# Keys carried between chunks through DRAM, and a fifth place for weight pairs

## The chip, the cores and the metric

The kernel runs on one core of a Trainium2 chip. The metric is the device time of one execution in microseconds (us), the median of three runs. One more execution of the same program was recorded by the hardware profiler; every duration below comes from that recording.

The core's engines run side by side, each through its own instructions in a fixed order: TensorE (PE, with its weight loads as PEld), VectorE (DVE), ScalarE (ACT), GpSimd (POOL), and SyncE (SP), which here only issues DMAs. An engine that waits for something holds up all that stands behind it in its own order.

## The reference

Two decoder layers over one sequence of 2048 tokens of width 1024. Each layer projects the stream once and splits the result; a sliding-window attention group and a Mamba-2 group read it side by side; both are gated, joined by one output projection, added to the stream and normalized.

```python
def hybrid_layer(x, w_in, conv_w, conv_b, dt_bias, a_log, d_skip, ssm_norm_w, sinks, w_out, ln_g, ln_b):
    proj = jnp.einsum("bld,de->ble", x, w_in)
    q, k, v, z_attn, z_ssm, xbc, dt_raw = jnp.split(proj, IN_SPLITS, axis=-1)
    attn = sliding_window_attention(q, k, v, sinks) * jax.nn.silu(z_attn)
    xbc = jax.nn.silu(causal_depthwise_conv(xbc, conv_w, conv_b))
    ...
    y = ssd_chunked(xs, dt, a, bm, cm)
    ssm = gated_rmsnorm(y, z_ssm, ssm_norm_w)
    out = jnp.einsum("ble,ed->bld", jnp.concatenate([attn, ssm], axis=-1), w_out)
    return layer_norm(DEEPNORM_ALPHA * x + out, ln_g, ln_b)
```

In the attention, queries and keys stand in blocks of 128 tokens, and a block of queries sees its own block of keys and the one before it. There are 4 key/value heads of 64 numbers a token. So a block of 128 keys is needed once more by the block that follows.

## The kernel before

**Tiles and stages.** The sequence is cut into 4 chunks of 512 tokens (4 blocks of 128), and the program walks layer by layer, chunk by chunk. In a chunk come the value projection (`stage_v`), then, for each of two halves: keys (`stage_k`), queries and gate of two heads (`proj_a`), attention block by block (`mix_a`), the projections of the Mamba group (`proj_s`), the output projection of the attention half (`out_proj`), the chunked scan block by block (`mix_s`), and, a half later, the output projection of the scan's half (the `late` list).

**Split numbers.** Every large product is made in three matmuls of rounded parts: a number is split into a high and a low part, and high x high, high x low and low x high are added up. A weight tile is thus a pair: `wpair`, 128 partitions x 2 x 512 numbers, 4 KB on each partition. It takes part in 12 matmuls (of 512 columns, or 272 for the value weights) and is then done with.

**Where weights come from.** On first use a weight is loaded raw (`wr`), split by ACT and DVE and written to DRAM as a pair; layer 1's weights are split ahead of time during chunks 1 to 3 of layer 0 (`w_ahead`, one for every third pair used). All later uses load the finished pair by one DMA of 512 KB (`w_split`, line 126). These loads go into a pool of 4 places: the load of a pair waits until the last matmul has read the pair that had its place four pairs earlier.

**Keys.** `stage_k` makes two tiles `kt` of 128 partitions x 2 (high, low) x 640 columns: 128 columns of the chunk before and 512 of its own. The 128 old columns come from `kcar`, four tiles of 1 KB a partition that live through the whole program: POOL copies `kcar` in (line 321, in chunks 1 to 3), ACT copies the last 128 columns out for the next chunk (line 326, in every chunk).

**Order.** The kernel is written through a scheduler: the code says what depends on what, and the scheduler, which models times of its own, sets each engine's order. Any change in the pools can move instructions all over. All DMAs are issued by SP from one queue, in one order. In PSUM the tags decide who shares a bank: `ps_g` (the transposed result of a scan block) and `ps_s` (scores) share one single bank under tag "s"; the projections share 5 banks.

Of the kernel before, what the change touches and what calls it, by code (L numbers as in the profile page):

```python
# [23 lines left out]
F32 = mybir.dt.float32  # L24
F32R = mybir.dt.float32r
# [6 lines left out]
P = 128  # L32
# [3 lines left out]
CH = 512  # L36
NCH = SEQ // CH
# [5 lines left out]
WP = 512  # L43
# [12 lines left out]
def trunk(ctx, tc, a):  # L56
    nc = tc.nc
    PS = bass.MemoryType.PSUM

    const = ctx.enter_context(tc.tile_pool(name="const", bufs=1))  # L60
    lay = ctx.enter_context(tc.tile_pool(name="lay", bufs=2))
    xp = ctx.enter_context(tc.tile_pool(name="xp", bufs=1))
    wp = ctx.enter_context(tc.tile_pool(name="wp", bufs=1))
# [4 lines left out]
    dram = ctx.enter_context(tc.tile_pool(name="dram", bufs=1, space=bass.MemoryType.DRAM))  # L68
# [4 lines left out]
    def bank(pool, name):  # L73
        if pool is ps_pj:
            return pool.tile([P, 512], F32, name=name, tag="bank")
        tag = TAG[name]
        return pool.tile([P, 512], F32, name=name, tag=tag, bufs=NS if tag == "s" else 1)
# [6 lines left out]
    def w_load(src, n, t=None):  # L84
        if t is None:
            t = wp.tile([P, WP], F32, name="wr", bufs=4)
        t = t[:, 0:n]
        nc.sync.dma_start(out=t if len(src.shape) == 2 else t.rearrange("p (k n) -> p k n", k=src.shape[1]), in_=src)
        return t

    kcar = [const.tile([P, 2, P], F32R, name=f"kc{i}") for i in range(4)]
    state = [const.tile([P, 512], F32, name=f"st{i}") for i in range(2)]
    halo = const.tile([P, 12, 3], F32, name="halo")

# [12 lines left out]
    def w_parts(hs, ls, src, scale, eng):  # L107
        if scale is None:
            split(hs, ls, src, "act", eng)
        else:  # L110
            nc.scalar.activation(out=hs, in_=src, func=AF.Copy, scale=scale)
            nc.vector.scalar_tensor_tensor(out=ls, in0=src, scalar=scale, in1=hs.bitcast(F32),
                                           op0=ALU.mult, op1=ALU.subtract)

    def w_store(key, n):
        w_dram[key] = dram.tile([P, 2, n], F32, name="wd_" + "_".join(map(str, key)))
        return w_dram[key]

    def w_split(key, c, dsrc, n, scale=None, pool=False, dst=None):

        if dst is None:
            dst = wp.tile([P, 2, WP], F32R, name="wpair", bufs=4)
        d = dst[:, :, 0:n]
        hs, ls = d[:, 0], d[:, 1]
        if key in w_dram:
            nc.sync.dma_start(out=d.bitcast(F32), in_=w_dram[key])
            cnt["use"] += 1
            if cnt["use"] % 3 == 0 and ahead:
                w_ahead(*ahead.pop(0))
            return hs, ls  # L130
        src = w_load(dsrc, n)
        cnt["w"] += pool
        w_parts(hs, ls, src, scale, nc.gpsimd if pool and cnt["w"] % 2 == 0 else nc.vector)
        if key[1] > 0 or not on_use(key):
            nc.sync.dma_start(out=w_store(key, n), in_=d.bitcast(F32))
        return hs, ls

    def on_use(key):
        return key[0] == "o" and key[2] > 1

    def w_ahead(key, dsrc, n, scale):

        src = w_load(dsrc, n)
        hi = wp.tile([P, WP], F32R, name="whi", tag="wr", bufs=4)[:, 0:n]
        w_parts(hi, src, src, scale, nc.vector)
        dst = w_store(key, n)
        nc.sync.dma_start(out=dst[:, 0], in_=hi.bitcast(F32))
        nc.sync.dma_start(out=dst[:, 1], in_=src)
# [80 lines left out]
    def proj_cm(X, L, i, ps, pool=True):  # L229
        for half in range(2):  # L230
            wh, wl = w_split(("cm", L, i, half), X.c, a["wcm"][L, i][:, half * 4:half * 4 + 4, :], 512, pool=pool)
            for kk in range(4):
                k = half * 4 + kk
                xh, xl = X[k]
                s = slice(kk * P, (kk + 1) * P)
                nc.tensor.matmul(out=ps, lhsT=wh[:, s], rhs=xh, start=(k == 0), stop=False)  # L236
                nc.tensor.matmul(out=ps, lhsT=wh[:, s], rhs=xl, start=False, stop=False)  # L237
                nc.tensor.matmul(out=ps, lhsT=wl[:, s], rhs=xh, start=False, stop=(k == KT - 1))  # L238
# [9 lines left out]
    def stage_v(L, X):  # L248
        banks = [bank(ps_acc, "ps_v") for _ in range(NB)]
        for k in range(KT):  # L250
            X[k]
            wh, wl = w_split(("v", L, k), X.c, a["wvdt"][L][:, k, :], 272)
            proj_tok(X, [t[:, 0:272] for t in banks], k, wh, wl)
        return banks
# [56 lines left out]
    def stage_k(L, c, pr, X):  # L311
        ps = bank(ps_cm, "ps_k")
        proj_cm(X, L, pr, ps, pool=False)
        kts = []
        for i in range(2):
            kv = 2 * pr + i
            kt = ap_.tile([P, 2, P + CH], F32R, name="kt", bufs=2)
            kf = kt.bitcast(F32)
            s, o = (slice(0, 64), slice(64, 128)) if i == 0 else (slice(64, 128), slice(0, 64))
            if c > 0:  # L320
                nc.gpsimd.tensor_copy(out=kt[:, :, 0:P], in_=kcar[kv].bitcast(F32))
            nc.scalar.copy(out=kt[s, 0, P:], in_=ps[s])
            nc.vector.tensor_tensor(out=kt[s, 1, P:], in0=ps[s], in1=kf[s, 0, P:], op=ALU.subtract)
            nc.scalar.copy(out=kt[o, 0, P:], in_=ps[s])
            nc.vector.tensor_copy(out=kt[o, 1, P:], in_=kf[s, 1, P:])
            nc.scalar.copy(out=kcar[kv], in_=kf[:, :, CH:CH + P])
            kts.append(kt)
        return kts

# [122 lines left out]
    def out_proj(L, c, grp, mixt, racc, evac, nw=None, pre=None, dhs=2):  # L452
        for dh in range(dhs):
            if pre is not None:
                pre(dh)
            banks = [bank(ps_acc, "ps_out") for _ in range(NB)]
            for e in range(4):
                wh, wl = w_split(("o", L, grp, dh, e), c, a["wo"][L, grp, dh][:, e, :], 512,
                                 None if nw is None else nw[:, e:e + 1])
                for b in range(NB):  # L460
                    mh, ml = mixt[b][:, 0, e, :], mixt[b][:, 1, e, :]
                    nc.tensor.matmul(out=banks[b], lhsT=mh, rhs=wh, start=(e == 0), stop=False)  # L462
                    nc.tensor.matmul(out=banks[b], lhsT=mh, rhs=wl, start=False, stop=False)  # L463
                    nc.tensor.matmul(out=banks[b], lhsT=ml, rhs=wh, start=False, stop=(e == 3))  # L464
            for b in range(NB):
                evac(b, racc[b][:, dh * 512:(dh + 1) * 512], banks[b])
# [251 lines left out]
    for L in range(DEPTH):  # L718
# [3 lines left out]
        for c in range(NCH):  # L722
# [7 lines left out]
            for half in range(2):  # L730
                kts = stage_k(L, c, half, X)
                qs, zs = proj_a(L, half * 2, X)
                flush()
                if half == 0:
                    racc = load_res(L, c)
                mixt = new_mixt()
                mix_a(L, lc, c, half * 2, vr, vprev, kts[0], qs, zs, mixt)
                qs, zs = proj_a(L, half * 2 + 1, X)
                mix_a(L, lc, c, half * 2 + 1, vr, vprev, kts[1], qs, zs, mixt)
                o = proj_s(L, lc, c, half, X, d)  # L740
                pre = None
                if half == 1 and (L, c) != (DEPTH - 1, NCH - 1):
                    Xn = XLoad(L + (c + 1) // NCH, (c + 1) % NCH)
                    pre = Xn.half
                out_proj(L, c, half, mixt, racc, ev_alpha if half == 0 else ev_add, pre=pre)
                mixt = new_mixt()
                rstd = mix_s(L, lc, c, half, d, o, mixt)

                def tail(L=L, c=c, half=half, mixt=mixt, racc=racc, rstd=rstd, lc=lc):
                    end = half == 1 and L == DEPTH - 1 and c == NCH - 1  # L750
                    nw = lc["nw"][:, half * 4:half * 4 + 4]
                    out_proj(L, c, 2 + half, mixt, racc, ev_rstd(rstd), nw, dhs=1 if end else 2)
                    if end:
                        last_out(L, c, 2 + half, mixt, racc, rstd, nw)
                    elif half == 1:
                        norm_store(L, c, racc)

                late.append(tail)
# [60 lines left out]
```

## Time and profile before

| | |
|---|---|
| median of 3 runs | 3217.2 us (3206.6, 3217.2, 3219.31) |
| profiled execution, whole | 3223.33 us |
| profiled execution, span from first to last instruction | 3221.6 us |
| TensorE busy | 3112.8 us (97%) |
| mean granted TensorE clock | 0.989 of full speed |
| DVE / ACT / POOL busy | 2165.2 / 1451.0 / 1241.2 us |
| DMA | 663.47 MB, mean 206 GB/s |

A "wait" of TensorE is idle time ahead of a matmul that ended when another engine or a DMA set a semaphore; the list of waits adds these up by matmul and by what ended them. An idle time that several things could have ended is put down to the last of them. Matmuls overlap in the engine, and the recording models their ends: a matmul of 512 columns is shown with 0.39 us, though the next one starts some 0.23 us after it. The granted clock is 1.00 when TensorE runs at its full 2.4 GHz, and a stretch that shows less has spent part of its time at 1.2 GHz.

### The profile page before, as it was taken

What the parts mean: (1) busy time and instruction counts of PE and PEld (TensorE: products, weight loads), DVE (VectorE), ACT (ScalarE), POOL (GpSimd) and SP (SyncE); (2) the same over time, 40 slices, a digit from 0 to 9 for tenths busy, and PEclk for the clock granted to TensorE, in tenths of its full rate; (3) what the DMA queues carried; (4) which work ended last, traced back from release to release, by engine and by line L of the source; (5) the groups of instructions that cost most, each with busy time, mean ns of one, the idle gap of its engine ahead of it and who ended that gap; (6) DMA issues with size and microseconds to landing.
All of it is one profiled execution on the core that took longest, in us unless ns stands there. A gap on an engine that the chain in (4) does not pass through costs nothing.

```text
span 3221.6 us, 46673 instructions
## 1 busy us (share of the span) xinstructions
PE 3112.8 (97%) x15448; PEld 2580.1 (80%) x15448; DVE 2165.2 (67%) x4687; ACT 1451.0 (45%) x4039; POOL 1241.2 (39%) x1455
## 2 busy tenths in 40 slices
PE   8999899899999999999999999999999999999996
PEld 7878787777877778877888888888888888888885
DVE  5867767567686686866758566675765757676475
ACT  5646535345354453544435444352542535335351
POOL 2443434414345143441425424343254433444224
PEclk9999999999999999999999999999999999999997
DMA  8756749487495774967546556665557545565461
GB/s 308 237 171 236 247 152 319 163 273 233 148 309 201 259 239 153 320 202 247 188 149 229 170 192 194 220 207 169 170 179 235 175 160 184 171 227 178 157 198 67
DMA packets 254450, 663.47 MB, mean 206 GB/s; under 512 B 28288, under 2 KB 49408, under 8 KB 254208
## 3 DMA queue, kind: packets, MB, share of 16 engines
q1 hardware_dynamic: 254208, 660.49, 61.9%
q8 instruction: 122, 2.00, 0.2%
q14 instruction: 120, 0.98, 0.1%
HBM read 534.02 MB, written 126.35 MB: 205 GB/s over the span
## 4 chain that ended last, share of the span: by engine, by line
PE 76%; DMA 13%; DVE 4%; POOL 2%; ACT 2%; issue 2%; SPq 1%; DVEq 0%; ACTq 0%; POOLq 0%
PE ps_out L462 6%; PE ps_out L464 6%; PE ps_out L463 6%; PE ps_xbc L238 4%; PE ps_xbc L236 4%; PE ps_xbc L237 4%; PE ps_z L237 3%; PE ps_z L238 3%; PE ps_z L236 3%; PE ps_q L236 3%; PE ps_yd L562 3%; PE ps_q L238 3%; PE ps_q L237 3%; DMA wr<-wcm 3%; DMA e<-a 3%; PE ps_zs L244 3%
## 5 line engine op out<-in xcount | busy, mean ns | idle before, releaser
L462 PE MATMUL ps_out<-wpair,mixt 128*128 128x512 f32 x1008 | 395.1, 401 | 24.2 <-DMA wpair<-wd_o 16.5
L464 PE MATMUL ps_out<-wpair,mixt 128*128 128x512 f32 x1008 | 396.4, 396 | 5.1 <-DVE mixt L105 4.7
L463 PE MATMUL ps_out<-wpair,mixt 128*128 128x512 f32 x1008 | 397.4, 394 | 0.5 <-DVE wpair L105 0.5
L236 PE MATMUL ps_xbc<-xh,wpair 128*128 128x512 f32 x768 | 307.5, 400 | 2.6 <-DMA wpair<-wd_cm 2.6
L237 PE MATMUL ps_xbc<-xl,wpair 128*128 128x512 f32 x768 | 302.7, 394 | 0.0
L238 PE MATMUL ps_xbc<-xh,wpair 128*128 128x512 f32 x768 | 302.3, 394 | 0.0
L404 ACT ACTIVATE e<-e,nm 128x129 f32<-128x129 f32 x512 | 203.1, 398 | 217.6 <-DVE nm L400 214.3
L555 ACT ACTIVATE e<-e,nacs 128x128 f32<-128x128 f32 x512 | 163.9, 391 | 226.3 <-DVE e L553 224.9
L462 PEld LDWEIGHTS ps_out<-wpair,mixt 128*128 128x128 f32 x1008 | 191.8, 191 | 69.4 <-DMA wpair<-wd_o 20.3
L464 PEld LDWEIGHTS ps_out<-wpair,mixt 128*128 128x128 f32 x1008 | 192.1, 191 | 47.8 <-DVE mixt L105 6.0
L463 PEld LDWEIGHTS ps_out<-wpair,mixt 128*128 128x128 f32 x1008 | 192.0, 190 | 39.8 <-DVE wpair L105 0.6
L507 DVE SCALAR_TENSOR_TENSOR cacc<-ps_xbc,conv,cacc 128x511 f32<-128x511 f32 (+2 forms) x288 | 213.1, 740 | 9.1 <-ACT cacc L504 7.0
L244 PE MATMUL ps_zs<-wpair,xh 128*128 128x512 f32 x512 | 205.0, 401 | 7.0 <-DMA wpair<-wd_z 7.0
L400 DVE CUSTOM_DVE_ANT_0 e<-e,bias 128x129 f32<-128x129 f32 x512 | 197.6, 422 | 10.8 <-DMA bias<-bias 5.7
L238 PE MATMUL ps_z<-xh,wpair 128*128 128x512 f32 x512 | 203.0, 396 | 0.0
L423 POOL TENSOR_SCALAR_AFFINE_SELECT gh<-fh 128x512 fp32r<-128x512 f32 x128 | 90.1, 704 | 292.0 <-ACT fh L100 284.5
L236 PE MATMUL ps_q<-xh,wpair 128*128 128x512 f32 x512 | 201.0, 393 | 1.0 <-DMA wpair<-wd_cm 1.0
L237 PE MATMUL ps_z<-xl,wpair 128*128 128x512 f32 x512 | 202.0, 395 | 0.0
L236 PE MATMUL ps_z<-xh,wpair 128*128 128x512 f32 x512 | 201.7, 394 | 0.0
L245 PE MATMUL ps_zs<-wpair,xh 128*128 128x512 f32 x512 | 201.7, 394 | 0.0
L246 PE MATMUL ps_zs<-wpair,xl 128*128 128x512 f32 x512 | 201.6, 395 | 0.0
L238 PE MATMUL ps_q<-xh,wpair 128*128 128x512 f32 x512 | 201.0, 393 | 0.0
(220 smaller groups left out, 8008.8 us busy)
## 6 DMA issues: line engine op xcount, KB each, us to landing
wpair<-wd_cm SPq DMA_DIRECT2D x420, 512.0 KB, 3.7
wpair<-wd_o SPq DMA_DIRECT2D x157, 512.0 KB, 4.1
wpair<-wd_z SPq DMA_DIRECT2D x112, 512.0 KB, 4.3
e<-a SPq DMA_DIRECT2D x128, 256.0 KB, 4.0
wr<-wcm SPq DMA_DIRECT2D x120, 256.0 KB, 4.6
wd_cm<-wpair SPq DMA_DIRECT2D x60, 512.0 KB, 3.5
wr<-wo SPq DMA_DIRECT2D x112, 256.0 KB, 4.7
wd_o<-wpair SPq DMA_DIRECT2D x32, 512.0 KB, 3.8
```

The costliest lines, as they stand in the source:

```text
L236: nc.tensor.matmul(out=ps, lhsT=wh[:, s], rhs=xh, start=(k == 0), stop=False)
L237: nc.tensor.matmul(out=ps, lhsT=wh[:, s], rhs=xl, start=False, stop=False)
L238: nc.tensor.matmul(out=ps, lhsT=wl[:, s], rhs=xh, start=False, stop=(k == KT - 1))
L244: nc.tensor.matmul(out=banks[b], lhsT=xh[:, s], rhs=wh, start=(k == 0), stop=False)
L245: nc.tensor.matmul(out=banks[b], lhsT=xh[:, s], rhs=wl, start=False, stop=False)
L246: nc.tensor.matmul(out=banks[b], lhsT=xl[:, s], rhs=wh, start=False, stop=(k == KT - 1))
L400: nc.vector.tensor_tensor_reduce(out=s5[:, h, :], in0=s5[:, h, :], in1=bias[:, h, :], scale=1.0, scalar=3.0e38, op0=ALU.add, op1=ALU.min, ...
L404: nc.scalar.activation(out=s5[:, h, :], in_=s5[:, h, :], func=AF.Exp, scale=-1.0, bias=nm[:, h:h + 1], accum_out=den[:, h:h + 1])
L462: nc.tensor.matmul(out=banks[b], lhsT=mh, rhs=wh, start=(e == 0), stop=False)
L463: nc.tensor.matmul(out=banks[b], lhsT=mh, rhs=wl, start=False, stop=False)
L464: nc.tensor.matmul(out=banks[b], lhsT=ml, rhs=wh, start=False, stop=(e == 3))
L507: nc.vector.scalar_tensor_tensor(out=acc[:, m:], in0=ps[:, 0:CH - m], scalar=cw[:, j:j + 1], in1=acc[:, m:], op0=ALU.mult, op1=ALU.add)
```

## The change

The carried keys no longer stay in SBUF. Each of the four heads gets two small DRAM tensors, used in turn by odd and even chunks. A chunk's end writes 128 columns there by a DMA (128 KB, not after the last chunk); the next chunk reads them by a DMA straight into the first columns of its `kt`. The POOL copy and the ACT copy go. The 4 KB a partition that `kcar` took hold a fifth place for `wpair`.

```diff
-    kcar = [const.tile([P, 2, P], F32R, name=f"kc{i}") for i in range(4)]
+    k_dram = [[dram.tile([P, 2, P], F32, name=f"k{kv}_{i}") for i in range(2)] for kv in range(4)]
...
         if dst is None:
-            dst = wp.tile([P, 2, WP], F32R, name="wpair", bufs=4)
+            dst = wp.tile([P, 2, WP], F32R, name="wpair", bufs=5)
...
             if c > 0:
-                nc.gpsimd.tensor_copy(out=kt[:, :, 0:P], in_=kcar[kv].bitcast(F32))
+                nc.sync.dma_start(out=kf[:, :, 0:P], in_=k_dram[kv][(c + 1) % 2])
...
-            nc.scalar.copy(out=kcar[kv], in_=kf[:, :, CH:CH + P])
+            if c < NCH - 1:
+                nc.sync.dma_start(out=k_dram[kv][c % 2], in_=kf[:, :, CH:CH + P])
```

All lines behind line 325 stand one further down in the changed kernel. Since the scheduler sets the order anew, about a quarter of TensorE's rows move. Two places follow.

**SP, layer 1, where the keys' DMAs now stand.** Before, the queue around the loads of four weight pairs of the Mamba projections, and then around those of the attention's projections of the next chunk (`wd_cm_...` are pairs in DRAM, `bias` the attention's distance table):

```order
L126 DMA wpair_23327<-wd_cm_1_24_1_13811 128x1024
L369 DMA bias_22982<-bias 128x516
L126 DMA wpair_23361<-wd_cm_1_25_0_13904 128x1024
...
L126 DMA wpair_24400<-wd_cm_1_10_0_6412 128x1024
L126 DMA wpair_24414<-wd_cm_1_10_1_6468 128x1024
```

The same places now:

```order
L321 DMA kt_24316<-k0_1_100 128x2x128
L126 DMA wpair_23361<-wd_cm_1_25_0_13906 128x1024
L370 DMA bias_22982<-bias 128x516
L126 DMA wpair_23375<-wd_cm_1_25_1_13978 128x1024
...
L126 DMA wpair_24400<-wd_cm_1_10_0_6416 128x1024
L327 DMA k0_0_99<-kt_24316 256x1x128
L327 DMA k1_0_101<-kt_24323 256x1x128
L126 DMA wpair_24414<-wd_cm_1_10_1_6472 128x1024
```

The load of the old keys (`kt_24316<-k0`) is issued in the half before the one that uses them, as soon as their tile is free; the two writes stand between two loads of weight pairs, just behind the making of the keys.

**TensorE, layer 1, chunk 1, the last scan block of the first half.** `ps_g` are the four transposes of the block's result, which ACT and DVE split into `mixt_22038`; the output projection of that block (`ps_out_22475`) reads it. `ps_st` is the scan's state, `ps_s` are scores of the next attention half. Before, from the transposes on (the rows left out are 18 more matmuls of the blocks `ps_out_22472` to `ps_out_22474`):

```order
L603 MATMUL ps_g_22285<-ident_310,yy_22256 128x128 x4
L464 MATMUL ps_out_22473<-wpair_22490,mixt_22036 128x512
L462 MATMUL ps_out_22474<-wpair_22490,mixt_22037 128x512
L463 MATMUL ps_out_22474<-wpair_22490,mixt_22037 128x512
...
L464 MATMUL ps_out_22474<-wpair_22518,mixt_22037 128x512
L462 MATMUL ps_out_22475<-wpair_22476,mixt_22038 128x512
L463 MATMUL ps_out_22475<-wpair_22476,mixt_22038 128x512
L464 MATMUL ps_out_22475<-wpair_22476,mixt_22038 128x512
```

Now:

```order
L590 MATMUL ps_st_22276<-fh_22272,bth_21485 128x512
L591 MATMUL ps_st_22276<-fl_22273,bth_21485 128x512
L592 MATMUL ps_st_22276<-fh_22272,btl_21486 128x512
L604 MATMUL ps_g_22285<-ident_314,yy_22256 128x128 x4
L388 MATMUL ps_s_22611<-kt_22325,q_22369 128x192 x2
L388 MATMUL ps_s_22611<-kt_22325,q_22403 128x192 x2
L463 MATMUL ps_out_22475<-wpair_22476,mixt_22038 128x512
L464 MATMUL ps_out_22475<-wpair_22476,mixt_22038 128x512
L465 MATMUL ps_out_22475<-wpair_22476,mixt_22038 128x512
```

Before, 22 matmuls of other blocks stand between the transposes and the first reader of `mixt_22038`; now four short score matmuls do.

## Rows read from the trace of the kernel before

**Rows 1.** The page's head: the span, and busy time by engine.
```profile
span 3221.6 us, 46673 instructions
PE 3112.8 (97%) x15448; PEld 2580.1 (80%) x15448; DVE 2165.2 (67%) x4687; ACT 1451.0 (45%) x4039; POOL 1241.2 (39%) x1455
```

**Rows 2.** Waits of TensorE, whole span: us in total, times, longest us.
```profile
PE ps_out L462 <- DMA wpair<-wd_o: 16.5, 11, 3.9
...
PE ps_zs L244 <- DMA wpair<-wd_z: 7.0, 8, 1.6
...
PE ps_out L464 <- DVE mixt L105: 4.7, 3, 2.1
...
PE ps_v L244 <- DMA wpair<-wd_v: 4.2, 4, 2.5
PE ps_out L462 <- ACT mixt L100: 2.7, 4, 0.7
...
PE ps_xbc L236 <- DMA wpair<-wd_cm: 2.6, 6, 0.8
...
PE ps_k L236 <- DMA wpair<-wd_cm: 1.2, 1, 1.2
PE ps_q L236 <- DMA wpair<-wd_cm: 1.0, 1, 1.0
```

**Rows 3.** The same list for layer 1 alone, 1640 us to the end.
```profile
PE ps_out L462 <- DMA wpair<-wd_o: 3.8, 3, 1.4
```

**Rows 4.** DMA issues: times, KB each, median us from issue to landing.
```profile
wpair<-wd_o SPq DMA_DIRECT2D x157, 512.0 KB, 4.1
...
bias<-bias SPq DMA_DIRECT2D x32, 258.0 KB, 3.7
...
a<-acsT SPq DMA_DIRECT2D x8, 32.0 KB, 2.0
```

**Rows 5.** TensorE's timeline, layer 1: start us, us, instruction, idle before it.
```profile
2238.76 0.39 PE L464 MATMUL ps_out<-wpair,mixt 128*128 128x512 f32 x1
2238.99 0.58 PE L387 MATMUL ps_s<-kt,q 128*128 128x192 f32 x4
2240.87 0.50 PE L462 MATMUL ps_out<-wpair,mixt 128*128 128x512 f32 x1 [1.29 <-DMA wpair<-wd_o]
```

**Rows 6.** Stretches: us; busy by engine, granted clock, DMA share, GB/s.
```profile
540.00:560.00 20.00, 18.51 (x96) 15.21 (x95) 13.28 (x36) 13.19 (x42) 7.12 (x11) 1.00 0.98 334
580.00:600.00 20.00, 17.75 (x73) 14.60 (x74) 9.06 (x14) 6.61 (x19) 8.33 (x9) 0.83 0.30 97
1044.00:1064.00 20.00, 17.22 (x72) 13.61 (x72) 12.49 (x23) 7.67 (x16) 5.10 (x5) 0.91 0.18 55
1380.00:1400.00 20.00, 16.97 (x77) 13.98 (x76) 13.74 (x22) 8.00 (x22) 9.06 (x10) 0.91 0.81 270
```

**Rows 7.** TensorE's timeline at the last scan block, layer 0, chunk 2.
```profile
1050.45 0.60 PE L603 MATMUL ps_g<-ident,yy 128*128 128x128 f32 x4
1051.73 0.50 PE L462 MATMUL ps_out<-wpair,mixt 128*128 128x512 f32 x1 [0.69 <-ACT mixt L100]
...
1054.56 0.79 PE L464 MATMUL ps_out<-wpair,mixt 128*128 128x512 f32 x1 [2.10 <-DVE mixt L105]
```

**Rows 8.** Tile `mixt`: duration ns min/median/max, first and last start us, forms.
```profile
L100 ACT CAST mixt<-ps_g x64: 574/587/589, 181.8 to 3187.5; 128x512 fp32r<-128x512 f32 x64
L105 DVE TENSOR_TENSOR mixt<-ps_g,mixt x64: 676/690/693, 184.3 to 3188.1; 128x512 fp32r<-128x512 f32 x64
```

**Rows 9.** Tile `kc`, the carried keys: the same columns.
```profile
L326 ACT CAST kc<-kt x32: 398/407/411, 33.7 to 2980.5; 128x256 fp32r<-128x256 f32 x32
L321 POOL CAST kt<-kc x24: 388/397/845, 286.7 to 2929.5; 128x256 fp32r<-128x256 f32 x24
```

**Rows 10.** Waits of SP's queue: us in total, times, longest us.
```profile
SPq L369 <- DVE nm L400: 55.9, 20, 5.1
```

## The prediction

> **What bounds the kernel now.** I read the page's head first. TensorE is busy for 3112.8 of 3221.6 us [rows 1]; 109 us of idle time, and what its clock loses, is all that a change of buffers can touch. The list of TensorE's waits, read next, says what ends that idle time: six of its rows name a weight pair that a DMA had not yet landed, 16.5 + 7.0 + 4.2 + 2.6 + 1.2 + 1.0 = 32.5 us [rows 2]. The same list cut at 1640 us gives layer 1 only 3.8 us of them [rows 3] and the single wait of `ps_q` [rows 2], 4.8 us in all, so 27.7 us lie in layer 0, where weights are also loaded raw, split and written back. Third came the stretches, for the clock and for how full the DMA engines are [rows 6]; fourth TensorE's timeline at one wait of each kind [rows 5, 7]; last the order of the changed program.
>
> Rows 5 show how such a wait arises. Matmuls of 512 columns start 0.23 us apart, so a pair with its 12 matmuls lasts 12 x 0.23 = 2.7 us, and a load takes 4.1 us from issue to landing [rows 4]. At 2237 us all four resident pairs are used side by side and end almost together. From the last matmul of the first of them to the first reader of the next pair the order has 9 matmuls and four short score matmuls: 9 x 0.23 + 0.45 = 2.5 us of work to hide the load, and TensorE stands for 1.29 us.
>
> **Part 1, the fifth place.** It lets each load be issued one pair earlier, so it gains up to 2.7 us of cover. At the place of rows 5 the next pair already has the fifth place, and the one after it has 21 matmuls and the scores ahead of it, 5.2 us. I counted this way over all 745 pair loads of both orders, from the matmul that frees a place to the first reader: the smallest cover rises from 2.0 to 4.8 us, and loads with under 4.1 us (the landing time) fall from 15 to none. In layer 1 all 4.8 us of waiting should go. In layer 0 a load can take longer, where the DMA engines are full: 98% busy at 334 GB/s between 540 and 560 us [rows 6]. While they stay full, the next pairs are late again, and 2.7 us is won once per such stretch rather than at every wait. Bounds for layer 0: nothing won, or all 27.7 us. The longest wait is 3.9 us [rows 2], and 2.7 us would take most of any one by itself, so I lean to the upper end and take two thirds, 18.5 us. Together -23.3 us.
>
> The clock follows. In the stretches from 580 and from 1380 us, where the longest two of these waits lie, the granted clock is 0.83 and 0.91 [rows 6]: 20 x 0.17 = 3.4 and 20 x 0.09 = 1.8 us lost at 1.2 GHz. If these two waits shrink by 2.7 us, both losses should go: -5.2 us; the bounds are 0 and that.
>
> The Trainium skill ("HBM Reference", section Specifications) gives a core about 358 GB/s when both cores of a pair stream, and about 425 GB/s when one streams alone. By the first figure 334 GB/s is near the end, and layer 0 would keep its 27.7 us; by the second there is room, and they could go. The trace's 98% busy at 334 GB/s stands nearer to the first.
>
> **Part 2, the order of the scan's last block.** This is what the diff does not tell. Once per chunk, at the end of the first half's scan, the last block's transposes `ps_g` are split by ACT (587 ns) and DVE (690 ns) [rows 8] before the output projection can read them. Rows 7 show the price where little stands between: 0.69 us for the high part, then 2.10 us for the low part. Over the run the list has three such waits on DVE, 4.7 us, and four on ACT, 2.7 us [rows 2]: 4.7 / 3 + 2.7 / 4 = 2.2 us a place. In the order of before three of the eight chunks have such a tight place, all in layer 0; elsewhere other blocks' matmuls fill it, 22 of them in the place printed above. In the new order all eight are tight, because pairs that arrive earlier let those matmuls run earlier. In the printed one the filling is gone, and `ps_s` needs the very bank that `ps_g` holds until both splits have read it. So five new stalls: 5 x 2.2 = +11 us. Bounds for one: 1.3 us (the two durations of rows 8 in a row) and 2.8 us (rows 7), so 6.5 to 14.
>
> The clock again: in the 20 us around the stall of rows 7 it is 0.91 [rows 6], 1.8 us lost. Five new ones cost between 0 and 9 us; I take two thirds, +6 us.
>
> **Part 3, the carry.** Removed are 32 ACT copies of 407 ns (13.0 us) and 24 POOL copies of 397 ns (9.5 us) [rows 9], on engines busy 45% and 39% of the span [rows 1]; behind them stands other work of ACT and POOL that no late matmul of rows 2 needs at that point. I cost them at nothing, at most 1 us gained. Added are 24 loads and 24 writes of 128 KB. No row shows that size; 32 KB land in 2.0 us and 258 KB in 3.7 us [rows 4]. Each load stands in the order 126 to 160 us of TensorE's work ahead of its first reader, so the latency is hidden; each waits for a matmul that comes before the one which the next pair's load waits for anyway, so nothing behind it in SP's queue is held. The writes wait for ACT and DVE to finish the keys, and pair loads stand behind them. The nearest waiting load, `bias`, holds the queue 55.9 / 20 = 2.8 us at a time [rows 10]; the pairs behind have covers of 12 to 14 us here. What is left is traffic: 48 x 131 KB = 6.3 MB, half of it in layer 0, where 3.1 MB at 334 GB/s are 9.4 us of full engines. That is the upper bound and 1 us below zero the lower; I take +1 us, since the engines are full for a small share of the time only.
>
> **The sum.** -23.3 - 5.2 + 11 + 6 + 1 = -10.5 us. The profiled execution took 3223.3 us, 1.7 more than its span, and would take 3212.8. It lies 6.1 us above the median of the three runs, and for a median I take the same step from there: 3217.2 - 10.5, about 3207 us.
>
> **Rivals.**
> - All pair waits go and the tight places are cheap. For it: no cover is left under 4.8 us. Against it: the full engines in layer 0, and rows 7. -32.5 - 5.2 + 6.5 = -31 us, 3186 us.
> - Slower: the tight places decide. Layer 0's waits stay because its DMA engines are full and a fifth place only fills sooner, while all five new stalls cost what rows 7 cost, clock included: -4.8 + 14 + 9 + 1 = +19 us, 3236 us. At that price of the stalls it is slower as soon as layer 0 gives back less than 19 of its 27.7 us. For it: 98% busy [rows 6]. Against it: only some stretches are that full; the one from 580 us, with the longest wait, shows 0.30. (The skill's 358 GB/s would give this one.)
> - The carry holds the queue: if a third of the 24 writes pass their 2.8 us on to TensorE, 8 x 2.8 = 22 us come on top of the forecast, 3229 us. For it: one queue, one order. Against it: the covers behind them.
>
> **How the numbers follow.** Forecast 0.57, all waits gone 0.25, slower 0.13, carry 0.05. A measurement of this kernel can tell about 0.5%, 16 us, from no change: faster means under 3201 us, slower over 3233. The first rival is faster; the forecast's own range, 3195 to 3222 (layer 0 giving half to all, stalls at 1.3 to 2.8 us), lies under 3201 for about an eighth of its chance: 0.25 + 0.07 = 0.32. Slower is the second rival, 0.13. The rest, 0.55, is no change that can be told. From 3187 to 3232 us less than 2 in 10 is left out: half of the first rival's tail below, and most of the second above.
>
> **What would show it.** In the changed profile: waits on `wpair<-wd_o` and `wpair<-wd_cm` gone in layer 1, and the six rows together at 9 us instead of 32.5; a stall at each of the eight chunks' first-half ends, on `ps_s` or `ps_out` with DVE or ACT as releaser, four of them in layer 1 where rows 3's list has none in those places now; the granted clock no longer low from 580 and from 1380 us but low at some of those stalls; `kt<-k` loads landing in 2 to 4 us and waited for by nobody. I am wrong if layer 0 keeps more than 15 us of pair waits, if the new stalls cost under 1 us each, or if SP's list names the key writes ahead of late pairs.

## The result, and the profile after

The changed kernel takes 3189.0 us (median of 4 runs, 3185.8 to 3194.7) where the kernel before takes 3215.1 beside it (4 runs). The ratio is 0.9924, 95% interval 0.9898 to 0.9950: 0.76% faster, more than the 0.5% that the prediction held to be as much as a measurement of this kernel can tell. Measured again, it was 0.9926 (0.9910 to 0.9941). The point of the prediction, 3207, was 18 us too high; the time lies 2 us inside its range, near the first rival's 3186.

The head of the page after, against [rows 1]:

```profile
span 3193.0 us, 46770 instructions
PE 3106.2 (97%) x15448; PEld 2580.1 (81%) x15448; DVE 2171.0 (68%) x4687; ACT 1435.2 (45%) x4007; POOL 1232.6 (39%) x1431
```

The span is 28.6 us shorter, and TensorE's busy time only 6.6 us of that. Its list of waits for the whole span (us in total, times, longest us), to be held against [rows 2]:

```profile
PE ps_st L591 <- DVE fl L105: 10.1, 11, 4.1
PE ps_o L431 <- POOL gh L424: 7.4, 5, 2.0
...
PE ps_s L388 <- DVE mixt L105: 7.0, 5, 1.4
...
PE ps_v L244 <- DMA wpair<-wd_v: 3.4, 1, 3.4
...
PE ps_o L432 <- POOL gl L424: 2.8, 3, 1.0
PE ps_out L463 <- ACT mixt L100: 2.7, 4, 0.7
...
PE ps_k L236 <- DMA wpair<-wd_cm: 1.8, 1, 1.8
...
PE ps_out L463 <- DMA wpair<-wd_o: 0.2, 1, 0.2
```

The six rows on pairs that DMA had not yet landed are now three, 3.4 + 1.8 + 0.2 = 5.4 us instead of 32.5. In layer 1 none is left; all of [rows 3] is gone. In their place stand DVE and POOL, the engines that prepare what TensorE reads next: `gh` and `gl` cost 10.2 us, `fl` 10.1.

The waits on `mixt` are the tight places of the prediction (and one wait of 0.7 us at the run's end, which was there before). Five of the eight look like this one at the end of a first half in layer 1 (TensorE's timeline):

```profile
2600.30 0.66 PE L604 MATMUL ps_g<-ident,yy 128*128 128x128 f32 x4 [0.39 <-POOL yy L599]
2602.36 0.69 PE L388 MATMUL ps_s<-kt,q 128*128 128x192 f32 x4 [1.40 <-DVE mixt L105]
```

1.40 us is ACT's and DVE's split, one after the other (587 and 690 ns in [rows 8]), and hardly more. DVE splits here as soon as ACT is done, and evicts output after it:

```profile
2601.61 0.69 DVE L105 TENSOR_TENSOR mixt<-ps_g,mixt 128x512 fp32r<-128x512 f32 x1 [0.41 <-ACT mixt L100]
...
2603.01 2.07 DVE L694 SCALAR_TENSOR_TENSOR racc<-ps_out,rstd,racc 128x512 f32<-128x512 f32 x3
```

At the place of [rows 7] DVE's order before was the other way round, three evictions and a gate's product ahead of the split, and TensorE waited 2.10 us for all of it:

```profile
1051.25 2.06 DVE L693 SCALAR_TENSOR_TENSOR racc<-ps_out,rstd,racc 128x512 f32<-128x512 f32 x3
1053.23 0.67 DVE L333 SCALAR_TENSOR_TENSOR zsa<-th,ps_z 128x512 f32<-128x512 f32 x1
1053.82 0.68 DVE L105 TENSOR_TENSOR mixt<-ps_g,mixt 128x512 fp32r<-128x512 f32 x1
```

The other three places cost 0.68 us each: there 21 to 24 output matmuls stand between the transposes and the scores and cover DVE's split. Stretches of the same run around such places, and where the two longest pair waits were (us; busy by engine; granted clock, DMA share, GB/s), against [rows 6]:

```profile
540.00:560.00 20.00, 19.25 (x98) 15.48 (x97) 13.30 (x36) 12.49 (x40) 7.00 (x10) 1.00 0.93 325
575.00:595.00 20.00, 18.59 (x83) 15.16 (x82) 11.78 (x16) 5.98 (x18) 12.93 (x13) 0.91 0.61 201
1035.00:1055.00 20.00, 16.64 (x63) 12.85 (x63) 11.09 (x23) 7.36 (x16) 5.12 (x5) 0.83 0.26 73
1375.00:1395.00 20.00, 18.24 (x89) 14.51 (x88) 12.58 (x19) 6.97 (x20) 10.68 (x10) 1.00 0.88 306
2593.00:2613.00 20.00, 18.21 (x93) 14.92 (x92) 11.78 (x27) 5.62 (x18) 6.33 (x7) 1.00 0.38 133
2982.00:3002.00 20.00, 17.82 (x85) 14.50 (x84) 9.17 (x24) 4.86 (x16) 3.97 (x5) 0.91 0.39 130
```

The low clock has moved, not gone. From 575 and 1375 us it is better than in [rows 6]. From 1035 us, the old tight place of [rows 7], it is 0.83 for 0.91; there a wait of 1.7 us on POOL's `yy` stands just before the 1.40. From 2982 us it is 0.91, where the same place had 1.00 before. Over the whole span the granted clock is 0.989 before and after.

The prediction did not look at the run's end. DVE's timeline before, where it evicts the last output groups; the lines from 3198.92 are the last four:

```profile
3193.25 0.75 DVE L693 SCALAR_TENSOR_TENSOR racc<-ps_out,rstd,racc 128x512 f32<-128x512 f32 x1 [0.91 <-PE ps_out L464]
3198.92 1.43 DVE L693 SCALAR_TENSOR_TENSOR racc<-ps_out,rstd,racc 128x512 f32<-128x512 f32 x2 [4.92 <-PE ps_out L661]
...
3200.86 0.73 DVE L693 SCALAR_TENSOR_TENSOR racc<-ps_out,rstd,racc 128x512 f32<-128x512 f32 x1
...
3202.22 0.70 DVE L693 SCALAR_TENSOR_TENSOR racc<-ps_out,rstd,racc 128x512 f32<-128x512 f32 x1
```

And after, the same four:

```profile
3170.38 0.73 DVE L694 SCALAR_TENSOR_TENSOR racc<-ps_out,rstd,racc 128x512 f32<-128x512 f32 x1
...
3175.02 0.74 DVE L694 SCALAR_TENSOR_TENSOR racc<-ps_out,rstd,racc 128x512 f32<-128x512 f32 x1
...
3179.10 0.73 DVE L694 SCALAR_TENSOR_TENSOR racc<-ps_out,rstd,racc 128x512 f32<-128x512 f32 x1
...
3181.08 0.73 DVE L694 SCALAR_TENSOR_TENSOR racc<-ps_out,rstd,racc 128x512 f32<-128x512 f32 x1
```

Before, the last of the run's weight pairs got a place only late (SP's queue):

```profile
3191.20 0.32 SPq L126 DMA_DIRECT2D wpair<-wd_o  x1
```

So TensorE did the parts of all four groups that need the other pairs, the four evictions start within 3.3 us of each other, and DVE idles 4.92 us and then has all evictions and norms at once: 19.57 us from TensorE's last matmul to the end. After, that load is issued by 3128 us, the groups end one by one over 10.7 us, DVE's norms go alongside, and 12.82 us are left.

The difference of the two profiled spans, by parts:

| part | before, us | after, us | change |
|---|---|---|---|
| TensorE idle, pairs from DMA | 32.6 | 5.4 | -27.2 |
| idle, splits of the transposes (`mixt<-ps_g`, DVE and ACT) | 7.4 | 9.7 | +2.3 |
| idle, all else between matmuls | 44.2 | 54.0 | +9.8 |
| TensorE busy | 3112.8 | 3106.2 | -6.6 |
| after the last matmul | 19.6 | 12.8 | -6.7 |
| before the first | 5.0 | 4.8 | -0.2 |

In a second profile of the changed kernel, at a mean granted clock of 0.994, the same rows are 8.1, 9.7, 57.8, 3095.8, 12.8 and 4.9 us. So the busy time differs by 10 us and the idle time by 7 between two runs of one program. The changes in the pair waits and in the run's end are well beyond that; the -6.6 of busy time is not.

The carry itself shows in the list of DMA issues (KB each, median us to landing); no matmul waits for it:

```profile
k<-kt SPq DMA_DIRECT2D x24, 128.0 KB, 2.4
kt<-k SPq DMA_DIRECT2D x24, 128.0 KB, 4.3
```

### The profile page after: what moved, and what is told of

It is laid out like the page before. It is cut to its first block, busy times and chain, and to the rows that moved or that the text cites. A ratio compares the mean times of both kernels' runs of the same rounds, so it can differ in the third digit from the quotient of the medians.

```text
span 3193.0 us, 46770 instructions
## 1 busy us (share of the span) xinstructions
PE 3106.2 (97%) x15448; PEld 2580.1 (81%) x15448; DVE 2171.0 (68%) x4687; ACT 1435.2 (45%) x4007; POOL 1232.6 (39%) x1431
## 4 chain that ended last, share of the span: by engine, by line
PE 75%; DMA 12%; DVE 6%; ACT 2%; issue 2%; POOL 2%; SPq 1%; POOLq 0%; DVEq 0%; ACTq 0%
PE ps_out L463 6%; PE ps_out L464 6%; PE ps_out L465 6%; PE ps_xbc L238 4%; PE ps_xbc L237 4%; PE ps_xbc L236 4%; DMA wr<-wcm 3%; PE ps_z L237 3%; PE ps_z L238 3%; PE ps_z L236 3%; DMA e<-a 3%; PE ps_q L238 3%; PE ps_q L237 3%; PE ps_q L236 3%; PE ps_yd L563 3%; PE ps_s L388 3%
## 5 line engine op out<-in xcount | busy, mean ns | idle before, releaser
L554 DVE TENSOR_TENSOR e<-e,nacs 128x512 f32<-128x512 f32 x128 | 118.0, 926 | 153.4 <-DMA e<-a 148.7
```

## The experiments

Theory A: the fifth place makes the gain, by pairs that land in time and by the run's end; the carry is worth about nothing. Ratios are to the kernel before, measured beside each run, with 95% intervals.

**Each half of the change alone.** First the carry in DRAM with four places (edit against the changed kernel):

```
-            dst = wp.tile([P, 2, WP], F32R, name="wpair", bufs=5)
+            dst = wp.tile([P, 2, WP], F32R, name="wpair", bufs=4)
```

> The keys go through DRAM, but the pair tile keeps its four places. Theory A (the fifth place makes the whole gain, the carry is worth about nothing): within 6 us of the kernel before, at a ratio of 0.998 to 1.002; TensorE's waits on weight pairs landing by DMA stay at 25 to 37 us, and 19 to 20 us pass after the last matmul. Rival B (56 copies fewer on ACT and POOL are what helps): at least 8 us faster, ratio under 0.9975, with pair waits unchanged. Rival C (the carry's DMAs crowd the queue and the fifth place pays for that too): at least 6 us slower, with pair waits over 37 us.

Measured: 0.9955 (0.9943 to 0.9968), some 14 us faster. Pair waits 28.8 us, 19.15 us after the last matmul, both as theory A has it; the time is not. All rows over 3 us on late pairs:

```profile
PE ps_out L463 <- DMA wpair<-wd_o: 19.3, 15, 5.0
...
PE ps_zs L244 <- DMA wpair<-wd_z: 3.9, 4, 1.6
PE ps_q L236 <- DMA wpair<-wd_cm: 3.8, 2, 2.4
```

Theory A's "about nothing" is refuted, and the number is rival B's. Then five places without DRAM (edit against the kernel before):

```
-    kcar = [const.tile([P, 2, P], F32R, name=f"kc{i}") for i in range(4)]
+    kcar = [const.tile([P, 2, P], BF16, name="kc")] * 4
...
-            dst = wp.tile([P, 2, WP], F32R, name="wpair", bufs=4)
+            dst = wp.tile([P, 2, WP], F32R, name="wpair", bufs=5)
...
-                nc.gpsimd.tensor_copy(out=kt[:, :, 0:P], in_=kcar[kv].bitcast(F32))
+                nc.gpsimd.tensor_copy(out=kt[:, :, 0:P], in_=kcar[kv])
```

> Five pair places, and no key goes through DRAM: the 32 ACT copies and 24 POOL copies of the kernel before stay, but all four key heads share one 16-bit tile in SBUF, so a chunk reads the keys of another head. Theory A: the same time as the changed kernel within 5 us, ratio to before 0.990 to 0.9945; pair waits on DMA under 10 us, 12 to 14 us after the last matmul. Rival B (half of the gain comes from the copies that went): ratio 0.995 to 0.998. Rival C (the carry costs in the changed kernel): ratio under 0.990.

Measured: 0.9895 (0.9879 to 0.9911), pair waits 7.1 us, 12.83 us after the last matmul. The fifth place alone gives all of the change's gain, so B does not hold for the whole. The ratio lies just under theory A's 0.990, on rival C's side; C is priced below. The two halves together would make 1.5% if they added; the change makes 0.75%. They do not add.

**The run's end alone.** The kernel before, its last pair in a free key tile:

```
-   dst=ap_.tile([P, 2, CH], F32R, name="q", bufs=3) if e < 3 else None))
+   dst=ap_.tile([P, 2, CH], F32R, name="q", bufs=3) if e < 3
+   else ap_.tile([P, 2, P + CH], F32R, name="kt", bufs=2)[:, :, 0:CH]))
```

> The kernel before with one edit: the last weight pair of the run goes to a free key tile instead of the ring of four pair places, so that it is loaded early and TensorE can finish the last four output groups one after the other. Theory A (6.8 of the 28.6 us are the run's end, where DVE's evictions no longer come in one burst): 5 to 7 us faster than before, ratio 0.9975 to 0.9985; the time after the last matmul falls from 19.6 to 12 to 14 us, and pair waits stay at 25 to 37 us. Rival D (the end's difference is a matter of the DVE's and POOL's own order, not of that pair): 17 us or more after the last matmul, ratio 0.9995 to 1.0005.

Measured: 0.9985 (0.9972 to 0.9998), 4.8 us, between 0.6 and 9. In the profile 12.84 us follow the last matmul instead of 19.57, with pair waits still at 30.1; DVE takes the last groups one by one, as after the change:

```profile
3198.40 0.75 DVE L694 SCALAR_TENSOR_TENSOR racc<-ps_out,rstd,racc 128x512 f32<-128x512 f32 x1
...
3202.49 0.73 DVE L694 SCALAR_TENSOR_TENSOR racc<-ps_out,rstd,racc 128x512 f32<-128x512 f32 x1
...
3204.47 0.73 DVE L694 SCALAR_TENSOR_TENSOR racc<-ps_out,rstd,racc 128x512 f32<-128x512 f32 x1
```

So the end is a part of the gain, and it hangs on that one pair. The edit leaves TensorE's order as it was but for 21 of 15448 rows, all behind 3190 us, so no new order of the rest stands behind the 4.8 us; how much of the 6.7 us they are, the interval leaves open.

**Why does the carry alone gain?** Two tests. One keeps the copies that the carry took away, on the same engines, beside the DMAs (four places; edit against the changed kernel):

```
+    kscr = [const.tile([P, 2, P], F32R, name=f"ks{i}") for i in range(4)]
...
+                nc.gpsimd.tensor_copy(out=kscr[kv], in_=kscr[kv].bitcast(F32))
...
+            nc.scalar.copy(out=kscr[kv], in_=kf[:, :, CH:CH + P])
```

> Keys through DRAM at four pair places, and the copies that this took away stay as well, on ACT and POOL, into a tile that nothing reads. Theory F (the carry alone is faster because ACT and POOL lose 56 copies): the gain goes, ratio to before 0.9985 to 1.0015. Theory G (it is the other order of layer 0 that comes with the edit, and the copies cost nothing): the ratio stays under 0.998 or goes somewhere else, in either direction, but not for reasons of ACT's or POOL's load.

The other changes only the order: in the kernel before, the POOL copy of the carried keys stands behind the four copies of the new ones.

```
-            if c > 0:
-                nc.gpsimd.tensor_copy(out=kt[:, :, 0:P], in_=kcar[kv].bitcast(F32))
...
             nc.vector.tensor_copy(out=kt[o, 1, P:], in_=kf[s, 1, P:])
+            if c > 0:
+                nc.gpsimd.tensor_copy(out=kt[:, :, 0:P], in_=kcar[kv].bitcast(F32))
```

> The kernel before with the same instructions; the POOL copy of the carried keys only stands three lines lower in the program, which changes some 600 rows of TensorE's order. Theory G (orders of equal work differ by several us in layer 0): 4 us or more away from before, either side, ratio under 0.9987 or over 1.0013. Theory F: no difference, 0.9990 to 1.0010.

Measured: 0.9945 (0.9929 to 0.9960) with the copies kept, so the load of the copies is not what gained; theory F falls. (The carried keys no longer wait for a POOL copy in either kernel; what that is worth was not tried.) The shaken order makes 0.9977 (0.9963 to 0.9990): 7 us from no instruction more or less. The edit moves some 750 of TensorE's 15448 rows, a third of them in layer 1; the carry alone moves some 2200. So one draw of a new order was worth 7 us; how far others go, one draw does not tell. Whether the carry's 14 us are such a draw or its own is open, but its profile says where they are not: layer 0 is 15.4 us shorter, and only 3.9 of that is idle time in gaps over 150 ns. The rest is TensorE's busy time, and the mean granted clock of the runs is 0.9912 against 0.9899 for the kernel before beside it (0.9913 against 0.9896 with the copies kept). At 3.2 us for a thousandth of the span, an estimate, 4 to 5 us of the gain go with the clock. Why the clock is higher there, nothing here shows.

A draw of that size does not explain the fifth place: five kernels that have it, each with an order of its own (the changed one, the one without DRAM and three below: the doubled carry, `ps_g` in bank `o`, and `e4` with three buffers), lie between 0.9895 and 0.9937. Two more with five places are slower; one also moves `ps_g` to bank `t`, the other also gives up a raw weight buffer.

**The carry priced on top of five places.** The changed kernel was run again, and once with every key write and load doubled:

```
+    k_two = [[dram.tile([P, 2, P], F32, name=f"j{kv}_{i}") for i in range(2)] for kv in range(4)]
...
+                nc.sync.dma_start(out=kf[:, :, 0:P], in_=k_two[kv][(c + 1) % 2])
...
+                nc.sync.dma_start(out=k_two[kv][c % 2], in_=kf[:, :, CH:CH + P])
```

> The changed kernel once more, beside the next three on one chip. Theory A (the fifth place makes the gain): ratio to before 0.9895 to 0.992, as far from before as the kernel with five places and no keys in DRAM (0.9895). If the carry added its own 0.45% to that: 0.984 to 0.987. If the carry costs: 0.993 to 0.996. A second profile of the same kernel also shows how far single waits differ from run to run: pair waits 3 to 9 us, time after the last matmul 12 to 14 us.

> The changed kernel with the carry doubled: each chunk writes its keys to two places in DRAM and the next loads both, one after the other, so 48 DMAs of 128 KB (6.3 MB) come on top. Theory A (the carry's DMAs cost about 1 us): ratio to before 0.990 to 0.995, that is the changed kernel's 0.9925 give or take the 0.25% that an order of equal work makes. Rival C (the carry costs the changed kernel the 0.3% by which the kernel with five places and no keys in DRAM is faster): twice of it, ratio 0.9945 to 0.9965, and more in layer 0 than in layer 1, with key loads landing over 6 us.

Measured: 0.9926 (0.9910 to 0.9941) again, and 0.9906 (0.9882 to 0.9930) with twice the traffic. The first lies between theory A's range and that of a carry that costs; the second is in theory A's. 6.3 MB more cost no time that can be told, so traffic is not seen to be why the kernel without DRAM is ahead of the changed one (0.9895 against 0.9926); that difference is of the size of one draw of the order. The waits do move: the doubled kernel has 15.0 us of pair waits, all in layer 0 and most of them in one row,

```profile
PE ps_out L466 <- DMA wpair<-wd_o: 9.5, 9, 2.1
```

where the two profiles of the changed kernel have 5.4 and 8.1. Whether that is the traffic or the new order is not shown; in the time it is not seen.

**Three places.**

```
-            dst = wp.tile([P, 2, WP], F32R, name="wpair", bufs=5)
+            dst = wp.tile([P, 2, WP], F32R, name="wpair", bufs=3)
```

> The changed kernel with three places for weight pairs instead of five. Counted from its order as the prediction counted (matmuls between the one that frees a place and the first reader, 0.227 us each, against the 4.1 us of a load), covers fall short by 20.3 us in layer 1, against 5.6 at four places and 0 at five. Theory A (a pair wait is the landing time less the cover): pair waits in layer 1 of 16 to 24 us (4.8 were measured at four places, none at five), in layer 0 of 35 to 60; ratio to before 1.006 to 1.02. Rival H (the scheduler hides a missing place by laying other work there, so places hardly matter): layer 1 under 8 us, ratio under 1.003.

Measured: 1.0032 (1.0019 to 1.0046). In layer 1 the list of waits reads:

```profile
PE ps_out L463 <- DMA wpair<-wd_o: 6.5, 8, 1.9
PE ps_xbc L236 <- DMA wpair<-wd_cm: 5.2, 8, 1.1
PE ps_zs L244 <- DMA wpair<-wd_z: 1.0, 1, 1.0
PE ps_k L236 <- DMA wpair<-wd_cm: 0.5, 2, 0.3
```

That is 13.2 us where the covers gave 20.3, between theory A's 16 to 24 and rival H's 8; the time too lies between their ranges. At four places it was 4.8 for 5.6, at five none for none. Counting covers told the direction and the place where waits end; at three places it overstated them by half, and why is not shown. Layer 0 has 39.8 us. With the carry in DRAM throughout, three, four and five places make 53.0, 28.8 and 5.4 us of pair waits but 1.0032, 0.9955 and 0.9925 in time: the last step takes 23 us of waits away and brings some 10 us.

**The tight places.** Two kernels give the transposes `ps_g` another bank:

```
-       "ps_g": "s"}
+       "ps_g": "t"}
```

> The changed kernel with one edit: the transposes ps_g use the bank of ps_st and ps_yd instead of that of the scores, so the scores behind the scan's last block need not wait until ACT and DVE have split it. Theory A (the eight tight places cost the changed kernel 9 us): the waits of ps_s on DVE mixt (7.0 us) go, and it is 3 to 9 us faster than the changed kernel, ratio to before 0.9895 to 0.9915. Rival E (the wait only moves, to ps_st and ps_yd, which then need ps_g's bank): those waits grow by 7 us or more, ratio 0.9925 to 0.997.

```
-       "ps_g": "s"}
+       "ps_g": "o"}
```

> The changed kernel with the transposes ps_g in the bank of ps_o and ps_yo instead of that of the scores. In its order 6 to 21 matmuls stand behind the scan's last block in every chunk, so the eight tight places are filled. Theory A (they cost 9 us in the changed kernel): waits of ps_s on DVE mixt and of ps_out on ACT mixt gone, 3 to 9 us faster than the changed kernel, ratio to before 0.987 to 0.9905. Rival E (as with the bank of ps_st: the wait moves to whoever shares the bank, here ps_o and ps_yo of the attention and the scan): those waits grow by more than 9 us, ratio over 0.993.

Measured: 1.0036 (1.0023 to 1.0049) and 0.9924 (0.9908 to 0.9940). With `t`, rival E's mechanism held: the bank is wanted by the scan itself, and TensorE's list names the new pairs of neighbours. The time is worse than E's range; the mean granted clock of these runs is 0.9876 against 0.9899 before.

```profile
PE ps_g L604 <- DVE st L598: 8.3, 11, 2.0
PE ps_yd L563 <- DVE mixt L105: 6.5, 4, 1.8
```

With `o`, the waits on the splits fell from 9.7 to 3.4 us and the time did not: theory A's 3 to 9 us did not come, nor did E's new waits. TensorE's idle time in sum, in gaps over 150 ns, is 74.8 us, against 73.3 and 80.3 in the two profiles of the changed kernel. The waits of `ps_pt` and `ps_s` on `e` are 19.6 us, against 8.4 and 15.9. That the matmuls which fill a tight place are then missing as cover elsewhere fits this, but only the unchanged sum is shown.

**Two tries at a faster version** keep the keys exact in SBUF in 2 KB (both halves of a key tile's partitions hold the same numbers, so half is stored) and take the other 2 KB from the fourth buffer of the scan's rows `e4`, or of the raw weights `wr` (against the kernel before; `wpair` at five places as well):

```
-    kcar = [const.tile([P, 2, P], F32R, name=f"kc{i}") for i in range(4)]
+    kcar = [const.tile([P, 2, P], F32R, name=f"kc{i}") for i in range(2)]
...
-                nc.gpsimd.tensor_copy(out=kt[:, :, 0:P], in_=kcar[kv].bitcast(F32))
+                for w in (s, o):
+                    nc.gpsimd.tensor_copy(out=kt[w, :, 0:P], in_=kcar[pr][s].bitcast(F32))
...
-            nc.scalar.copy(out=kcar[kv], in_=kf[:, :, CH:CH + P])
+            nc.scalar.copy(out=kcar[pr][s], in_=kf[s, :, CH:CH + P])
```

> A try at a faster version: five pair places and the keys in SBUF, exact, without DRAM. Both halves of a key tile's partitions hold the same numbers, so one half is kept and two heads share a tile, 2 KB instead of 4; POOL copies it back twice. The other 2 KB come from the scan's rows e4, which have three buffers instead of four. Theory A (five places make the gain, and the keys' trip through DRAM costs the changed kernel up to 0.3%): ratio to before 0.988 to 0.992. Rival (a buffer less for e4 makes the scan's rows come late, DVE waits for e<-a as it is): ratio 0.993 to 1.0, with more TensorE time spent waiting on e at ps_yd.

> The same, but the 2 KB come from the raw weight tile wr, which has three buffers instead of four. Theory A: ratio to before 0.988 to 0.992. Rival (layer 0 prepares the weights of both layers through wr, so a buffer less delays pairs there): ratio 0.993 to 1.003, with ACT-written pairs waited for in chunk 0 by more than 12 us (7.9 before) or stored pairs landing late.

Measured: 0.9937 (0.9925 to 0.9949) and 1.0056 (1.0040 to 1.0072). Neither beats the changed kernel. The first has its rival's time but not its sign, since no matmul of `ps_yd` waits on `e`; it is also within one draw of the changed kernel. The second shows that not every place is worth the same: with three raw buffers, TensorE idles 84.0 us in layer 0 (56.0 in the changed kernel, gaps over 150 ns). The pair that ACT writes from a raw weight is waited for 13.0 us, as its rival said, but the time is beyond the rival's range, the mean granted clock is 0.9867 against 0.9897 before, and the longest row is another:

```profile
PE ps_s L388 <- DVE e L397: 13.7, 12, 2.8
PE ps_out L463 <- DMA wpair<-wd_o: 11.4, 7, 3.3
PE ps_o L431 <- POOL gh L424: 10.7, 7, 4.7
```

No version with exact keys beat the changed kernel by more than the intervals.

## Why the prediction was right, and where it was off

- **The pair waits** were the right term. It took 23.3 us, all of layer 1 and two thirds of layer 0; 27.2 went, and layer 0 kept 5.4 of 27.7. The full DMA engines between 540 and 560 us (98% before, 93% at 325 GB/s now) did not bring the waits back. By the lower of the two figures of the Trainium skill ("HBM Reference", section Specifications), about 358 GB/s, the prediction had layer 0 keep its waits. That did not come here; no stretch shown reached either figure, so neither is tested.
- **The tight places** came where the order put them, eight of eight, four of them in layer 1, but this is the term that was mis-sized: 2.2 us a place, +11 us for five new ones. The five new ones cost 1.40 us three times and 0.68 twice, 5.6 us together, under the lower bound of 6.5; two of them meet the prediction's own sign of being wrong, under 1 us. The three old ones fell from 6.8 to 3.5 us, which it had taken to stay, so all such waits rose by 2.3. The 2.2 was a mean over the old places (1.8, 2.8 and 2.2 us), and at each of them DVE had two or three output evictions ahead of its split. It was the price of DVE's order there, not of a split. The lower bound for one place, the two splits one after the other, was what the row of durations showed.
- **The clock** terms, -5.2 and +6, came out as no change in sum (granted 0.989 in both). At the new place from 2982 us it is low, from 2593 it is not, and at the old one from 1035 it is lower than before; the single terms can't be told better than that from one run.
- **The run's end** was missed, 6.7 us. The order of the changed program showed it, and the prediction read the order only where pairs were waited for: the last pair is waited for by nobody, because the scheduler had put its readers last. What waits is DVE.
- **What is late next** was missed as well: +9.8 us of TensorE's idle time, above all on `gh`, `gl` and `fl`, which POOL and DVE write. The prediction named no successor for the removed waits but the tight places.
- **The carry** was costed at +1 us. Doubling it changes no time that can be told, and its loads land in 4.3 us with nobody waiting, a little more than the forecast 2 to 4. That the carry alone is 14 us faster at four places was not foreseen; half of that is the size of the one draw of an order, 4 to 5 us go with the clock, and the cause is open.

By these sizes the forecast's -10.5 becomes -27.2 + 2.3 - 6.7 + 9.8 = -21.8, and with TensorE's busy time and the start -28.6. A matmul that ends ahead of a gap is counted as busy with its whole 0.39 us, where in a dense row the next one starts 0.23 us after it. Gaps of any length fell from 108 to 82, so some 4 us of the 6.6 us of busy time may be that (an estimate, 26 x 0.16 us); the rest is within what two runs of one program differ by. The likeliest case, no change that can be told, was the wrong one, because the price of the tight places and the missing end both stood on the slow side. That the time is still inside the range, and 3 us from the first rival, is in part luck: neither has the run's end, the late successors or the busy time, and these three (-6.7, +9.8, -6.6) make -3.5 together.

## What to carry to other kernels

When a buffer is added, look for loads that the order has already given up on: a late load that nobody waits for has moved its readers, and its price stands on another engine, above all at the end of the run. Price a new stall from the durations of what it waits for, not from a mean of old stalls that had other causes. Where a scheduler may lay the program out anew at an edit, compare the orders, and change something neutral first: here that alone moved the time by 0.2%, and the parts of the change missed their sum by 0.75%.

## What the runs showed of the hardware

- The same stall in the same program is answered differently by the clock. In the first profile of the changed kernel the stretch 2982 to 3002 us is at 0.91; in the second one the same place, with the same two waits of 0.8 and 1.4 us, reads

```profile
2980.00:3000.00 20.00, 17.82 (x90) 14.61 (x89) 8.66 (x23) 4.86 (x16) 3.97 (x5) 1.00 0.47 152
```

- The spread of one kernel's times goes, loosely, with its mean granted clock: of 21 runs of the kernel before on one chip the fastest (span 3209.3 us) has 0.993, the two at 0.992 average 3213.0, the six at 0.989 3221.3 and the three at 0.988 3219.0. A thousandth of the clock is 3.2 us of this span, so the clock is to be read before two single runs are compared.
